# A decoder layer on one core: the first block's gate and up products taken together, the sum of squares later, and fewer steps in the recurrence

## The chip, the core and the metric

The kernel runs on one core of a Trainium2 chip. The metric is the time of one execution on the device in microseconds (us). Six parts of the core matter here. TensorE (PE) multiplies matrices, and its weight loads (PEld) overlap the products. VectorE (DVE) and ScalarE (ACT) work element by element. GpSimd (POOL) does small things and issues some transfers. SyncE (SP) issues most of the DMA transfers, in order. A transfer's landing is told to the engines by a semaphore.

## The reference, cut to what matters

A layer of 256 tokens and 2048 features in float32: a feed-forward part, a mixer that runs attention over a sliding window beside a recurrence (RWKV-7), an attention over a memory, a second feed-forward part, and a last norm. What the change touches:

```python
def rms_norm(x, g):
    return x * rsqrt(mean(x * x) + 1e-6) * g

def swiglu(h, w_gate, w_up, w_down):          # 2048 -> 5632 -> 2048
    return (silu(h @ w_gate) * (h @ w_up)) @ w_down

x = x + 0.5 * swiglu(rms_norm(x, ffn1_norm), ffn1_w_gate, ffn1_w_up, ffn1_w_down)
...
w_log = -softplus(-(w0 + tanh(xw) @ w2)) - 0.5      # decay of the recurrence
a = sigmoid(a0 + xa @ a2)
S = S * w_t + (S @ a_t) * b_t + v_t * k_t           # for each of 256 tokens, 16 heads of 64
y_t = S @ r_t
```

## The kernel before

**Products in three passes.** A float32 product is made of three TensorE products of split operands: each operand is a high part (rounded to TensorE's format, float32r) and a low part (the rest), and `times` (L428) multiplies weight high by feature high (L431), weight low by feature high (L432) and weight high by feature low (L433). Features are the operand that is loaded into TensorE (128 features by 128 tokens), weights stream by 512 columns. Tokens come in two halves, `t` 0 and 1.

**Weights.** `weight_plan` (L106) lists every product in order with its columns. A product is cut into items of two chunks (`KU`) of 128 rows. `load` (L294) issues an item's transfers on SP, `divide` (L362) splits it: ACT casts the high part (L333), DVE subtracts for the low part (L334). `next_item` (L381) issues loads some items ahead and splits up to two single items, or one paired item, ahead of use. A single item has one weight. A paired item has two weights in a tile `raw2` of four chunks, of which there are three buffers; outside the feed-forward's pairs, one such tile holds two single items.

**Two kinds of product.** `product` (L399) multiplies one weight into two banks, one for each half of the tokens. `product_pair` (L489) multiplies gate and up together into several banks; for the items in `SEVEN` it uses seven products in place of eight, of sums of the operands (`sums` L346, `combinations` L443), and for the others the plain eight. In before, the first block of 512 columns of each feed-forward part is two calls of `product` (L760 and L765: gate, then silu, then up, then the product of both), and all later blocks are `gate_up` (L560) by `product_pair`.

**The start.** PE multiplies ones eleven times (L201) until the first data are there. x comes transposed as `xT`, sixteen chunks of features in four tiles; `features` (L682) scales a chunk by the norm's gain and splits it on ACT (L688) and DVE (L689). When all are done, `squares` (L699) squares the four tiles on ACT (L703), adds them up on DVE (L706, L710), and multiplies by a column of ones on PE (L715) for the sum over features; `rstd` (L721) turns it into the scale that the silu and the gate need at the block's end.

**The order of the work.** The stream of weight products is written out in order. All else is in generators, which `Interleave` (L61) moves on by a step whenever the stream calls `tick`, every six products; a `yield` ends a step, `idle(n)` lets n ticks pass. The groups are stepped in a fixed order. The order in which the program states its operations is their rank. The compiler then puts each engine's instructions in order by that rank among those it thinks ready, and each engine works its own list in order. `by_turns` (L170) keeps a list of small products in order, and with `late` it ties them behind the newest product of the stream.

**The recurrence.** It is done in blocks of 128 tokens, `c` 0 and 1, and in two halves of the heads, `h`. `decay_and_rate` (L1054) makes decay and rate in four bursts of products (L1068), each with four sigmoids on ACT (L1079), with two idle ticks between bursts. `values` (L1240) multiplies the values (L1247) and, a step later, the bonus (L1255). `chain` (L1354) makes three masked products for each block (`masked`, L1379: products on PE at L177, then a mask on DVE at L1387), and between them `known`, `solved`, `turned`, `results`, the state of the second block (L1462, L1467), each a step on PE that needs the last one's result. `invert` (L1271) makes the inverse that `solved` needs, with many products of 32x32 and 64x64 (L1295). PSUM has four single banks (`acc`) and two double ones (`two`); masked products, transposes (L185) and the paired products p3, p5, p6 and p7 take double ones.

## Time and profile before

| what | value |
|---|---|
| time, median of 3 runs | 2233.66 us (2233.21 to 2236.87) |
| time of the profiled execution | 2233.47 us |
| its span, first to last instruction | 2231.7 us |
| mean granted clock of TensorE | 0.998 |
| weights' casts on ACT, L333 | 769, 763.4 us |
| weights' low parts on DVE, L334 | 770, 883.2 us |
| moved by DMA | 433.31 MB, mean 194 GB/s |

The span is what the profile's times count from. A row of the timeline gives start, duration, engine, line, operation, tiles (out<-in), shape and count, and in brackets the idle time before it and what ended it. A row of the waits gives who waited for whom, the total in us, the number of times, and the longest. Line numbers are those of the kernel before.

### The profile page before, as it was taken

Reading aid. Unit: us, or ns where it says so; the run is one execution under the profiler, and the core shown is the slowest. Engines: PE = TensorE matmul, PEld = TensorE weight load, DVE = VectorE, ACT = ScalarE, POOL = GpSimd, SP = SyncE. Lnnn points to the kernel's source line nnn. Section 1 sums busy time; section 2 is a strip of 40 time slices with the busy share of each in tenths; the row PEclk is TensorE's granted clock in tenths of the full one; section 3 lists DMA queues with packets and bytes.
Section 4 is the critical chain, followed back from the end, with each engine's and each line's share of the span. In section 5 each row is a group of like instructions: output and inputs, shape, how many; then the busy total and the mean of one; then the engine's idle time right before and its main releaser. Section 6 shows DMA issues by size and latency. Waiting matters only on the chain.

```text
span 2231.7 us, 28333 instructions
## 1 busy us (share of the span) xinstructions
PE 2216.3 (99%) x10792; PEld 1821.0 (82%) x10792; DVE 1747.3 (78%) x2038; ACT 1193.5 (53%) x1436; POOL 71.9 (3%) x139
## 2 busy tenths in 40 slices
PE   9999999999999999999999999999999999999998
PEld 7788888888888877888888888888888888888886
DVE  7988988898987567977545576558888988898987
ACT  6555555555555557544443445556555555555554
POOL 1000000000000000010400000001000000000000
PEclk9999999999999999999999999999999999999999
DMA  7666666565656545677624766657665665565664
GB/s 246 200 226 189 216 195 199 191 207 189 207 184 216 166 137 149 211 230 224 178 63 136 230 223 201 188 162 263 198 203 184 207 202 194 189 203 194 207 205 153
DMA packets 220424, 433.31 MB, mean 194 GB/s; under 512 B 13840, under 2 KB 16224, under 8 KB 220288
## 3 DMA queue, kind: packets, MB, share of 16 engines
q1 hardware_dynamic: 213088, 410.70, 57.9%
q0 software_dynamic: 6624, 20.14, 3.0%
q8 instruction: 84, 1.38, 0.3%
q10 hardware_dynamic: 576, 0.66, 0.1%
q14 instruction: 52, 0.43, 0.1%
HBM read 419.00 MB, written 12.45 MB: 193 GB/s over the span
## 4 chain that ended last, share of the span: by engine, by line
PE 93%; DVE 3%; DMA 1%; issue 1%; ACT 1%; SPq 0%; POOLq 0%; POOL 0%; DVEq 0%; ACTq 0%
PE acc L431 20%; PE acc L432 20%; PE acc L433 20%; PE two L431 8%; PE two L432 8%; PE two L433 8%; PE two L185 2%; DVE lo L334 1%; PE two L177 1%; DMA raw<-in_ffn_w_up_dram 1%; DMA raw<-in_ffn_w_gate_dram 1%; PE two L1295 0%; DVE tlo L359 0%; PE acc L1432 0%; PE acc L1397 0%
## 5 line engine op out<-in xcount | busy, mean ns | idle before, releaser
L333 ACT CAST hi<-raw 128x1024 fp32r<-128x1024 f32 (+1 forms) x769 | 763.4, 1002 | 792.0 <-PE acc L433 372.1
L334 DVE TENSOR_TENSOR lo<-raw,hi 128x1024 fp32r<-128x1024 f32 (+1 forms) x770 | 883.2, 1156 | 338.4 <-ACT hi L333 337.5
L431 PE MATMUL acc<-hi,xhi 128*128 128x512 f32 (+1 forms) x1256 | 493.4, 394 | 0.8 <-ACT xhi L688 0.7
L432 PE MATMUL acc<-lo,xhi 128*128 128x512 f32 (+1 forms) x1256 | 488.1, 389 | 1.2 <-DVE lo L334 1.1
L433 PE MATMUL acc<-hi,xlo 128*128 128x512 f32 (+1 forms) x1256 | 486.8, 388 | 0.0
L431 PEld LDWEIGHTS acc<-hi,xhi 128*128 128x128 f32 x1256 | 236.0, 188 | 56.1 <-issue 6.3
L432 PEld LDWEIGHTS acc<-lo,xhi 128*128 128x128 f32 x1256 | 236.1, 188 | 52.1 <-DVE lo L334 4.0
L433 PEld LDWEIGHTS acc<-hi,xlo 128*128 128x128 f32 x1256 | 236.1, 188 | 47.4
L359 DVE TENSOR_TENSOR tlo<-raw,thi 128x1024 fp32r<-128x1024 f32 x160 | 192.9, 1218 | 0.5 <-ACT thi L358 0.5
L358 ACT CAST thi<-raw 128x1024 fp32r<-128x1024 f32 x160 | 165.9, 1051 | 39.5 <-DVE raw L353 20.9
L432 PE MATMUL acc<-lo,hhi 128*128 128x512 f32 x424 | 166.4, 392 | 0.0
L433 PE MATMUL acc<-hi,hlo 128*128 128x512 f32 x424 | 165.2, 390 | 0.0
L431 PE MATMUL acc<-hi,hhi 128*128 128x512 f32 x424 | 159.9, 391 | 0.0
L431 PE MATMUL two<-hi,xhi 128*128 128x512 f32 x320 | 126.0, 394 | 0.0
L432 PE MATMUL two<-lo,xhi 128*128 128x512 f32 x320 | 124.7, 390 | 0.0
L433 PE MATMUL two<-hi,xlo 128*128 128x512 f32 x320 | 124.6, 389 | 0.0
L353 DVE TENSOR_TENSOR raw<-raw 128x1024 f32<-128x1024 f32 x80 | 97.5, 1219 | 18.5 <-DMA raw<-in_ffn_w_up_dram 16.2
L432 PEld LDWEIGHTS acc<-lo,hhi 128*128 128x128 f32 x424 | 79.6, 188 | 19.2 <-DVE lo L334 3.0
L431 PEld LDWEIGHTS acc<-hi,hhi 128*128 128x128 f32 x424 | 79.1, 188 | 18.7 <-ACT hi L333 2.6
L433 PEld LDWEIGHTS acc<-hi,hlo 128*128 128x128 f32 x424 | 79.6, 188 | 16.3
L431 PEld LDWEIGHTS two<-hi,xhi 128*128 128x128 f32 x320 | 60.1, 188 | 13.8 <-DVE u L583 0.4
L433 PEld LDWEIGHTS two<-hi,xlo 128*128 128x128 f32 x320 | 60.1, 188 | 12.6
(380 smaller groups left out, 3178.8 us busy)
## 6 DMA issues: line engine op xcount, KB each, us to landing
raw<-in_ffn_w_gate_dram SPq DMA_DIRECT2D x167, 512.0 KB, 3.9
raw<-in_ffn_w_up_dram SPq DMA_DIRECT2D x160, 512.0 KB, 4.8
raw<-in_ffn_w_down_dram SPq DMA_DIRECT2D x152, 512.0 KB, 4.8
raw<-in_w_in_dram SPq DMA_DIRECT2D x136, 512.0 KB, 4.0
raw<-in_w_out_dram SPq DMA_DIRECT2D x32, 512.0 KB, 4.2
raw<-in_ffn_w_down_dram SPq DMA_DIRECT2D x12, 1024.0 KB, 5.2
raw<-in_ffn_w_up_dram SPq DMA_DIRECT2D x8, 1024.0 KB, 7.2
raw<-in_w_proj_attn_dram SPq DMA_DIRECT2D x16, 512.0 KB, 4.1
```

What stands on the lines that cost most here:

```text
L177: prev = pe.matmul(to, lhs, rhs, **how)
L185: prev = pe.transpose(to, src, ident[:])
L333: newest["act"] = act.copy(hi[:, s], raw[:, s])
L334: newest["dve"] = dve.tensor_tensor(lo[:, s], raw[:, s], f32(hi[:, s]), ALU.subtract)
L353: dve.tensor_tensor(ta[:], raw[:, 1:3], raw[:, 0:2], ALU.subtract)
L358: act.copy(hi[:, s], t[:])
L359: dve.tensor_tensor(lo[:, s], t[:], f32(hi[:, s]), ALU.subtract)
L431: pe.matmul(o, xh, hi, start=first, stop=False, **how)
L432: pe.matmul(o, xh, lo, start=False, stop=False, **how)
L433: newest["pe"] = pe.matmul(o, xl, hi, start=False, stop=last, **how)
```

## The change

Four things change. The first feed-forward part's first block becomes one `product_pair` of gate and up, without the sevens (`first_block`); the second feed-forward part keeps its two products. Its first item is loaded in four pieces, in the order gate, up, gate, up; the other three loads of the start are whole paired items; the item-by-chunk order of the first single item goes. The multiplications by ones before the start are ten instead of eleven. In `squares` the last products come four steps after the fold instead of one, tied behind the newest product, for x in a double bank. In the recurrence, the idle ticks between the two bursts of a half's decay go (four follow them), the step between the two products of `values` goes, that between the first two masked products goes, and the second block's first masked product moves ahead of `results(0)`, beside `turned`, so that a step less follows it.

```diff
--- before.py
+++ after.py
@@ -87,12 +87,14 @@
         self.until(lambda: not any(q for _, q in self.groups.values()))
 
 
-def feed_forward_plan(wg, wu, wd):
+def feed_forward_plan(wg, wu, wd, together):
     for gi, (j0, nj) in enumerate(GROUPS):
         for j in range(j0, j0 + nj):
-            if j == 0:
+            if j == 0 and together:
+                yield (wg, wu), 0, KD, (0, 0), ()
+            elif j == 0:
                 for w in (wg, wu):
-                    yield w, 0, KD, j * 512, 512
+                    yield w, 0, KD, 0, 512
             else:
                 yield (wg, wu), 0, KD, (j * 512, j * 512), SEVEN
         for n in (0, 2):
@@ -107,7 +109,7 @@
 
 
     w = {n: v[0] for n, v in a.items() if "_w_" in n or n.startswith("w_")}
-    yield from feed_forward_plan(w["ffn1_w_gate"], w["ffn1_w_up"], w["ffn1_w_down"])
+    yield from feed_forward_plan(w["ffn1_w_gate"], w["ffn1_w_up"], w["ffn1_w_down"], True)
     yield None
     w_in = w["w_in"]
     cols = [ATTN_W, 0, 512]
@@ -134,7 +136,7 @@
     for n in range(4):
         yield w["w_cross_o"], 0, 4, n * 512, 512
     yield None
-    yield from feed_forward_plan(w["ffn2_w_gate"], w["ffn2_w_up"], w["ffn2_w_down"])
+    yield from feed_forward_plan(w["ffn2_w_gate"], w["ffn2_w_up"], w["ffn2_w_down"], False)
 
 
 @with_exitstack
@@ -198,7 +200,7 @@
 
     newest = {}
     idle_bank = acc()
-    for _ in range(11):
+    for _ in range(10):
         pe.matmul(idle_bank[:, :P], ones[:], ones[:], start=True, stop=True)
 
     def select(out, in_, pattern, op, fill, base, mult):
@@ -300,6 +302,14 @@
             raw = raws[i] = at["pool"].tile(
                 [P, 2 * KU, 512], F32, tag="raw2", name="raw2", bufs=RAW
             )
+            for j, queue in pieces or ():
+                if j is None:
+                    queue()
+                    continue
+                v, c, r = (w[j in (1, 2)], c0[j in (1, 2)], (k + j // 2) * P)
+                queue.dma_start(raw[:, j], v[r : r + P, c : c + 512])
+            if pieces:
+                return
             rows = slice(k * P, (k + KU) * P)
             for v, c, to in zip(w, c0, (raw[:, 0:4:3], raw[:, 1:3])):
                 newest["load"] = nc.sync.dma_start(
@@ -364,15 +374,16 @@
             return
         raw = raws[i]
         if not paired(i):
-            parts[i] = split_raw(raw, EACH if i < AHEAD else WHOLE, i == 0)
+            parts[i] = split_raw(raw, WHOLE)
         elif items[i][4]:
             t = sums(raw)
             u1, g1 = split_raw(raw[:, 2:4], WHOLE)
             g0, _ = split_raw(raw[:, 0:2], ONE)
             parts[i] = (g0, g1, u1), t
         else:
-            g0, u0 = split_raw(raw[:, 0:2], WHOLE)
-            u1, g1 = split_raw(raw[:, 2:4], WHOLE)
+            how = WHOLE if i else EACH
+            g0, u0 = split_raw(raw[:, 0:2], how, i == 0)
+            u1, g1 = split_raw(raw[:, 2:4], how)
             parts[i] = (g0, u0), (g1, u1)
 
     def cost(i):
@@ -410,12 +421,6 @@
         for k in range(0, nk - KU * len(skewed), KU):
             bg.until(lambda: all(k + i in x.done for i in range(KU)))
             u = next_item()
-            if at["item"] == 1:
-                for i in range(KU):
-                    for t in range(2):
-                        multiply(o[t][:, :n], x, u, k, t, nk, (i,))
-                    bg.tick()
-                continue
             for t in range(2):
                 multiply(o[t][:, :n], x, u, k, t, nk)
                 bg.tick()
@@ -432,9 +437,9 @@
         pe.matmul(o, xh, lo, start=False, stop=False, **how)
         newest["pe"] = pe.matmul(o, xl, hi, start=False, stop=last, **how)
 
-    def multiply(o, x, u, k, t, nk, chunks=range(KU)):
+    def multiply(o, x, u, k, t, nk):
         s = slice(t * P, (t + 1) * P)
-        for i in chunks:
+        for i in range(KU):
             times(
                 o, [x.at(p, k + i)[:, s] for p in range(2)], u[i],
                 k + i == 0, k + i == nk - 1,
@@ -588,6 +593,22 @@
         product_pair(x, c, w, False, SEVEN, EARLY, after, end, finish)
         return hb
 
+    def first_block(sp, x, norm, w):
+        hb = sp.tile([P, 2, 512], F32, tag="hb", name="hb", bufs=2)
+
+        def finish(to, b):
+            bg.until(lambda: norm.r is not None)
+            t = to in ("p4", "p5")
+            if to in ("p2", "p4"):
+                act.activation(hb[:, t], b[to], AF.Silu, scale=norm.r[t])
+            else:
+                dve.scalar_tensor_tensor(
+                    hb[:, t], b[to], norm.r[t], hb[:, t], ALU.mult, ALU.mult
+                )
+
+        product_pair(x, None, w, False, (), (), None, None, finish)
+        return hb
+
     def down(sp, h, c, w, xs, then):
 
 
@@ -708,14 +729,18 @@
                 return
             yield
             dve.tensor_tensor(total[:, :2], total[:, :2], total[:, 2:], ALU.add)
-            yield
-            b = acc()
-            for t in range(2):
-                for k in range(2):
-                    pe.matmul(
+            yield from idle(4)
+            b = two()[:, 0] if whole else acc()
+            by_turns(
+                [
+                    (
                         b[:, t : t + 1], total[:, k, t * P : (t + 1) * P], ones[:, :1],
-                        start=t + k == 0, stop=t + k == 2, skip_group_check=True,
+                        dict(start=t + k == 0, stop=t + k == 2, skip_group_check=True),
                     )
+                    for t in range(2) for k in range(2)
+                ],
+                late=True,
+            )
             self.r = rstd(b[:, :2].unsqueeze(2))
 
     def rstd(ss):
@@ -757,9 +782,14 @@
                     if j == j0 + nj - 1:
                         bg.spawn("feat", c["next"].pop())
                     continue
+                if not last:
+                    hb = first_block(sp, norm.x, norm, wg)
+                    bg.spawn("feat", transposed(hb, 0))
+                    continue
                 pg = product(norm.x, wg)
+                hb = sp.tile([P, 2, 512], F32, tag="hb", name="hb", bufs=2)
+
                 bg.until(lambda: norm.r is not None)
-                hb = sp.tile([P, 2, 512], F32, tag="hb", name="hb", bufs=2)
                 for t in range(2):
                     act.activation(hb[:, t, :], pg[t], AF.Silu, scale=norm.r[t])
                 pu = product(norm.x, wu)
@@ -820,22 +850,17 @@
         pair = sp.tile([P, 8, T], F32, tag="thi", name="xt")
         turned = [v[:] for v in turned] + [pair[:, :4], pair[:, 4:]]
         load(0, (
-            (slice(0, 1), nc.sync),
+            (0, nc.sync),
             (None, lambda: act.dma_start(turned[0][:, :1], a["xT"][:, :1])),
+            (1, nc.sync), (3, nc.sync),
             (None, lambda: nc.sync.dma_start(turned[0][:, 1:2], a["xT"][:, 1:2])),
-            (slice(1, 2), nc.sync), (slice(2, 4), nc.sync),
+            (2, nc.sync),
         ))
         act.copy(junk_t[:, :1], ones[:, :1])
         nc.sync.dma_start(turned[0][:, 2:], a["xT"][:, 2:4])
-        load(2, (
-            (slice(0, 2), nc.sync),
-            (None, lambda: nc.sync.dma_start(turned[1], a["xT"][:, 4:8])),
-            (slice(2, 4), nc.sync),
-        ))
-        for n in range(2, 4):
+        for n in range(1, 4):
+            load(n)
             nc.sync.dma_start(turned[n], a["xT"][:, 4 * n : 4 * n + 4])
-            if n < 3:
-                load(2 * n)
         for n in range(4):
             bg.spawn("feat", n1.features(n, turned[n], turned[0], True))
         bg.spawn("const", late_vectors())
@@ -1080,7 +1105,7 @@
                                 dst[:, q + i, :], b[:, e, i * T : (i + 1) * T], AF.Sigmoid,
                                 bias=bias[:, c : c + 1],
                             )
-                    yield from idle(2)
+                yield from idle(4)
             for h in range(2):
                 for c in range(4):
                     dve.tensor_tensor_scan(
@@ -1249,7 +1274,6 @@
                         start=True, stop=True,
                     )
             act.copy(vtok[h][:], b[:])
-            yield
             b = two()
             for i in range(2):
                 pe.matmul(
@@ -1445,7 +1469,6 @@
                 return t
 
             masked(0, 0)
-            yield
             masked(0, 1)
             yield from wait_for(f"inverse{h}")
             yield
@@ -1454,6 +1477,7 @@
             yield
             solved(0)
             bk = turned()
+            masked(1, 0)
             yield
             results(0)
             b = acc()
@@ -1465,8 +1489,6 @@
                     )
             s0 = wide("s0")
             dve.tensor_tensor(s0[:], b, decays[:], ALU.mult)
-            masked(1, 0)
-            yield
             masked(1, 1)
             yield
             known(1)
```

## The prediction

> **What bounds the kernel.** I read the page first: the busy shares, then the chain that ended last.
>
> ```profile
> span 2231.7 us, 28333 instructions
> PE 2216.3 (99%) x10792; PEld 1821.0 (82%) x10792; DVE 1747.3 (78%) x2038; ACT 1193.5 (53%) x1436; POOL 71.9 (3%) x139
> ...
> PE 93%; DVE 3%; DMA 1%; issue 1%; ACT 1%; SPq 0%; POOLq 0%; POOL 0%; DVEq 0%; ACTq 0%
> ```
>
> TensorE (PE) is busy for 99% of the span and is 93% of the chain. The change removes no product of the layer, so it can gain only where PE waits or loses its pace. Such places are short. Next I therefore read what PE waited for, in the first 62 us, where the first block lies.
>
> ```profile
> PE acc L715 <- DVE xt L710: 1.6, 1, 1.6
> PE acc L202 <- POOL ones L197: 1.1, 1, 1.1
> PE acc L432 <- DVE lo L334: 0.8, 2, 0.5
> PE acc L431 <- ACT xhi L688: 0.7, 1, 0.7
> ```
>
> The longest wait is the sum of squares (L715), then the weights' and features' parts. The last view is the order of time. The profiled run took 2233.47 us for its span of 2231.7, so 1.8 us lie around it; its time is 0.19 below the median of 2233.66. All sums below start from 2233.47.
>
> **The first block, start.** From the timeline of the first 30 us, all engines, then of PE alone:
>
> ```profile
> 1.06 4.99 PE L202 MATMUL acc<-ones 128*128 128x128 f32 x22 [1.06 <-POOL ones L197]
> ...
> 5.77 0.51 PE L431 MATMUL acc<-hi,xhi 128*128 128x512 f32 x1
> ...
> 11.13 1.05 ACT L333 CAST hi<-raw 128x1024 fp32r<-128x1024 f32 x1 [0.42 <-DMA raw<-in_ffn_w_gate_dram]
> ...
> 12.21 1.23 DVE L334 TENSOR_TENSOR lo<-raw,hi 128x1024 fp32r<-128x1024 f32 x1 [0.71 <-ACT hi L333]
> ...
> 12.69 1.71 ACT L688 ACTIVATE xhi<-xt,g_first 128x256 fp32r<-128x256 f32 x4 [0.51 <-DMA xt<-in_xT_dram]
> ...
> 13.26 0.50 PE L431 MATMUL acc<-hi,xhi 128*128 128x512 f32 x1
> ...
> 18.09 2.00 ACT L333 CAST hi<-raw 128x1024 fp32r<-128x1024 f32 x2 [1.08 <-DMA raw<-in_ffn_w_gate_dram]
> ```
>
> ```profile
> 28.45 0.39 PE L431 MATMUL acc<-hi,xhi 128*128 128x512 f32 x1
> 28.67 0.39 PE L432 MATMUL acc<-lo,xhi 128*128 128x512 f32 x1
> ```
>
> Between two products in full flow lie 28.67 - 28.45 = 0.22 us, over longer stretches 0.2275 (0.39 is a duration that overlaps the next). The block has 8 x 2 x 12 = 192 products in both versions. In before, an item (two chunks of one weight, 0.52 MB) feeds 12 products; afterwards an item is two chunks of both weights (1.05 MB) and feeds 24. The 25th product starts at 13.26 in before, the 85th at 28.45: 15.2 us for 60 products that take 13.65, so 1.5 us of waits lie between them, while loads and features arrive just in time.
>
> After the change the second item's first half is cast whole, from a gate chunk and an up chunk, so both of its transfers must have landed. Up to there 1.05 MB of the first item, 0.52 of features and 1.05 of the second item have to come, 2.62 MB. The rows show when before had as much: at 11.13 the wait for six gate chunks ends (with four of features 2.10 MB), at 12.69 that for four feature chunks more (2.62 MB). So: landed 12.7, cast 1.05, PE goes on at about 13.85. The low part (1.23) is ready at 15.1; eight of the half's twelve products use the high part alone, 1.8 us, so it comes in time. Then each item lasts 24 x 0.2275 = 5.46 us. The third item needs 4.19 MB; before had 4.72 at 18.09, which by the slope from 12.69 puts it at 16.8, ready at 17.9, wanted at 19.3. No wait from there on. The 85th product then starts at 13.85 + 60 x 0.2275 = 27.5, **0.95 us earlier** than in before. Neighbouring landings are 1.5 us apart, which I take as the error of 12.7: from 2.45 earlier to 0.55 later.
>
> The idle matmul less is 4.99/22 x 2 = 0.45 us by its two records. I cost it at nothing: PE starts earlier, and then waits for the second item all the same. If item two came early enough, its 0.45 would show; that is inside the bounds above. The item order on the loads' queue (SP) changes too: load four now waits there for the first item's buffer, ahead of the last features, but these are wanted by the seventh item, about 41 us.
>
> **The sum of squares.** From the timelines of PE and of DVE:
>
> ```profile
> 30.94 0.39 PE L433 MATMUL acc<-hi,xlo 128*128 128x512 f32 x1
> 32.92 1.05 PE L715 MATMUL acc<-ones,xt 128*128 128x1 f32 x8 [1.60 <-DVE xt L710]
> ```
>
> ```profile
> 32.19 0.68 DVE L710 TENSOR_TENSOR xt<-xt 128x512 f32<-128x512 f32 x1
> ```
>
> PE stands from 30.94 + 0.23 = 31.17 to 32.92, **1.75 us**. Everything behind L715 on PE, the whole weight stream, stood with it. Afterwards the eight matmuls come three steps of the background work later. A step is issued every six products, so 18 x 0.2275 = 4.1 us, and they are tied behind the newest product. In items they fall in the sixth, near 38 us, 5 us after the fold at L710 is done. The scale that follows is wanted only at the block's end, near 50 us. I take the whole 1.75; bounds 0 (DVE 5 us later) and 1.9. The same edit for the memory's norm meets no wait in before and is worth nothing.
>
> **The block's end.** PE, then windows (length, then busy us and records of PE, PEld, DVE, ACT, POOL, then granted clock, DMA share, GB/s), then DVE and SP:
>
> ```profile
> 55.73 0.61 PE L431 MATMUL acc<-hi,xhi 128*128 128x512 f32 x2
> 56.48 0.50 PE L432 MATMUL acc<-lo,xhi 128*128 128x512 f32 x1
> ```
>
> ```profile
> 35.00:40.00 5.00, 5.00 (x24) 4.12 (x23) 3.33 (x5) 3.38 (x6) 1.10 (x1) 1.00 0.27 104
> 40.00:45.00 5.00, 5.00 (x24) 4.14 (x23) 3.22 (x5) 1.75 (x2) 0.00 (x0) 1.00 0.66 210
> ...
> 44.00:62.00 18.00, 17.86 (x83) 14.42 (x82) 17.92 (x25) 9.73 (x11) 0.00 (x0) 1.00 0.60 190
> ```
>
> ```profile
> 45.37 1.23 DVE L353 TENSOR_TENSOR raw<-raw 128x1024 f32<-128x1024 f32 x1
> ```
>
> ```profile
> 40.56 0.46 SPq L305 DMA_DIRECT2D raw<-in_ffn_w_up_dram  x1
> ```
>
> At 55.73 two products take 0.75 instead of 0.455, and 0.1 more is lost behind them: 0.4 us, for DVE's low part. DVE is full from 44 to 62 (17.92 of 18) but idle for 3.4 us between 35 and 45: the first paired item with sums was issued only at 40.56, and its first DVE step ran at 45.37. With pairs from the start the buffer cycle is that of the later blocks, the load goes out when item six is split (about 35), and DVE can use that idle time. I take **0.4 gained**. The other bound is 1 us lost, since PE now arrives 3 us earlier at a stretch where DVE has no spare time, and the last up bank must be read before the next block gets it.
>
> **The joined steps.** PE's timeline, at the decay, then at the second half's masked products, then at the first half's:
>
> ```profile
> 840.80 0.39 PE L433 MATMUL acc<-hi,xlo 128*128 128x512 f32 x1
> 841.12 1.13 PE L177 MATMUL two<-xs,wa 64*128 64x256 f32 x8
> 842.19 0.50 PE L431 MATMUL acc<-hi,xhi 128*128 128x512 f32 x1
> 842.52 0.40 PE L432 MATMUL acc<-lo,xhi 128*128 128x512 f32 x1
> ```
>
> ```profile
> 1168.56 1.16 PE L177 MATMUL two<-at,aa 64*128 64x128 f32 x16
> 1171.23 1.16 PE L177 MATMUL two<-rt,aa 64*128 64x128 f32 x16
> ```
>
> ```profile
> 1112.39 1.16 PE L177 MATMUL two<-at,aa 64*128 64x128 f32 x16
> 1113.62 1.16 PE L177 MATMUL two<-rt,aa 64*128 64x128 f32 x16
> ```
>
> PE does not wait at these steps; it loses at each crossing between small products and the stream. A decay burst takes 842.52 - 840.80 - 2 x 0.2275 = 1.27 us, of which 842.19 - 841.12 = 1.07 is the burst: 0.20 is lost outside it. A masked product alone costs 1171.23 - 1168.56 - 6 x 0.2275 = 1.30; next to another 1.23. So a join saves 0.07 to some 0.35 (the outside loss and the inner entry). I take 0.25 for each of the two joins of the decay, 0.2 for each of three masked ones (the first half's first pair already stands side by side), 0.1 for each of two at the values: 0.5 + 0.6 + 0.2 = **1.3 us**, bounds 0.4 and 2.5. The eight sigmoids that now follow at once hold ACT, but weights are split two items, 5.5 us, ahead.
>
> **The sum.** 0.95 + 1.75 + 0.4 + 1.3 = 4.4 us. 2233.47 - 4.4 = 2229.1 us. What a measurement here can tell from no change is 0.2%, 4.5 us: faster means below 2229.2, slower above 2238.1. The forecast is a gain that lies on that line.
>
> **The rivals.** First, the start gives nothing: DVE, full from 44 us, holds PE where it stood, and the 3.1 us of the first three terms are waited out there. Then only the joins remain: 2233.47 - 1.3 = 2232.2. For it speaks 17.92 of 18, against it the 3.4 idle us before. Second, the joins save nothing, since PE's order follows readiness and not the steps: 2233.47 - 3.1 = 2230.4. The pair at 1112.39 shows steps that joined unasked. The others lie on the slow side or the fast side by the clock:
>
> ```profile
> 1135.66:1139.07 3.41, 3.41 (x60) 2.63 (x61) 1.23 (x1) 1.07 (x2) 0.89 (x2) 1.00 0.71 235
> 1139.07:1142.49 3.42, 3.42 (x89) 3.38 (x82) 0.99 (x2) 0.93 (x3) 0.00 (x0) 1.00 0.02 5
> 1142.49:1145.90 3.41, 3.41 (x15) 2.38 (x15) 0.53 (x2) 2.06 (x5) 0.00 (x0) 0.50 0.00 0
> 1145.90:1149.31 3.41, 3.41 (x49) 3.22 (x49) 1.23 (x1) 1.88 (x2) 0.00 (x0) 1.00 0.09 11
> ```
>
> In the recurrence the granted clock is 0.50 for one stretch of 3.41 us, just after one filled with small products. At half pace it costs up to 1.7 us. Third, the changed order avoids it, or item two lands early: 2229.1 - 1.7 = 2227.4. Fourth, **slower**: denser bursts, with fewer full products between them, lower the clock in more stretches. Before has one among the 35 stretches from 1092 to 1212; three more give 2234.2, slower than before, and six more 2239.3, slower by over 0.2%. [...]
>
> [...]
>
> **Chances.** The forecast 0.42, split evenly by the line; the third rival 0.24, faster; the first 0.16 and the second 0.11, within; the fourth 0.07, of which 0.05 is over the bound. With a little of the second below the line, faster is 0.48, the same 0.47, slower 0.05. The range goes from 2226.0 (the third with joins at their upper bound, 2227.4 - 1.2, rounded down) to 2233.5 (start and joins at nothing); the fourth and half of the tail below are left out.
>
> **What would show it.** The start: the second item's first product near 13.85, waiting for ACT's cast, and none after. The squares: L715 near 38 us, with no wait. The end: no product near 53 us waiting for L334. The joins: four decay bursts become two, and masked products stand beside transposes and each other. The clock: the count of stretches at 0.50. The prediction is wrong if item two lands after 14.5, if DVE's idle time between 35 and 45 stays, or if more clock stretches fall.

## The result, and the profile after

| what | before | after |
|---|---|---|
| time, median (lowest to highest) of 17 executions each | 2234.28 us (2231.03 to 2237.1) | 2229.66 us (2228.26 to 2231.34) |
| ratio, 95% interval | | 0.998, 0.9973 to 0.9988 |
| time and span of the profiled execution | 2233.47, 2231.7 us | 2228.26, 2226.5 us |

The changed kernel is 4.6 us faster; 2229.1 had been forecast. The total hides errors of both signs, so I read the profile of after in the same order. This profile is of the fastest of its 17 executions, so differences between the two profiles come out somewhat larger than those between the medians. In the changed kernel L343 is the cast of weights on ACT (L333 in before), L344 the low part on DVE (L334), and L436 to L438 are the three products (L431 to L433). Its page, busy time and chain first:

```profile
span 2226.5 us, 28338 instructions
...
PE 2212.4 (99%) x10790; PEld 1820.2 (82%) x10790; DVE 1746.7 (78%) x2038; ACT 1193.4 (54%) x1436; POOL 70.9 (3%) x139
...
PE 97%; DVE 1%; ACT 1%; DMA 0%; issue 0%; POOLq 0%; POOL 0%; SPq 0%; ACTq 0%; DVEq 0%
```

PE is still busy for 99% and is now 97% of the chain, so what changed is again to be found in short places. What PE waited for in the first 64 us (waiter, who was waited for, total, times, longest):

```profile
PE acc L436 <- ACT hi L343: 2.0, 2, 1.3
PE acc L204 <- POOL ones L199: 1.1, 1, 1.1
PE acc L437 <- DVE lo L344: 0.8, 2, 0.5
PE acc L436 <- ACT xhi L709: 0.3, 1, 0.3
```

The wait for the sum of squares is gone. The longest is now for ACT's cast of weights, twice. The timeline of PE says where:

```profile
5.72 0.50 PE L436 MATMUL acc<-hi,xhi 128*128 128x512 f32 x1 [0.33 <-ACT xhi L709]
...
12.80 0.73 PE L436 MATMUL acc<-hi,xhi 128*128 128x512 f32 x2 [1.27 <-ACT hi L343]
...
14.06 0.50 PE L437 MATMUL acc<-lo,xhi 128*128 128x512 f32 x1 [0.29 <-DVE lo L344]
...
27.11 0.39 PE L436 MATMUL acc<-hi,xhi 128*128 128x512 f32 x1
...
37.99 0.95 PE L179 MATMUL two<-ones,xt 128*128 128x1 f32 x8
...
54.82 0.74 PE L436 MATMUL acc<-hi,xhi 128*128 128x512 f32 x2 [0.70 <-ACT hi L343]
...
56.75 0.50 PE L437 MATMUL acc<-lo,xhi 128*128 128x512 f32 x1 [0.49 <-DVE lo L344]
...
839.13 2.00 PE L179 MATMUL two<-xs,wa 64*128 64x256 f32 x16
...
853.51 1.09 PE L187 MATMUL two<-ident,tok 128*128 128x128 f32 x8 [0.41 <-ACT tok L905]
...
1163.31 1.16 PE L179 MATMUL two<-at,aa 64*128 64x128 f32 x16
1164.31 1.06 PE L179 MATMUL two<-rt,aa 64*128 64x128 f32 x16
```

The second item's first product comes at 12.80, the 85th product at 27.11, the squares (now L179) at 37.99 without a wait, and the masked products stand side by side. New are two waits at the block's end (54.82 and 56.75), and one behind the joined decay (853.51).

The cleanest ledger is the start of one and the same instruction in two timelines. The table gives how much earlier (negative) it is than in before's profile, for after and for five experiments of the next section. "Product" counts the stream's 512-column products; the others are transposes on PE. An asterisk marks the interval in which a profile had a stretch of 3.41 us at half clock; before's own lies between 1086 and 1296.

| instruction, us in before | after | block only | joins only | no joins | no block | not late |
|---|---|---|---|---|---|---|
| 85th product, 28.45 | -1.34 | -1.31 | -0.27 | -1.02 | -0.36 | -0.93 |
| 145th product, 44.84 | -3.17 | -3.15 | +1.35* | -2.86 | -2.17 | -2.77 |
| transpose, 168.69 | -1.91 | -2.06 | +1.30 | -2.06 | +1.85* | -1.24 |
| transpose, 827.40 | -1.99 | -1.88 | +1.26 | -2.16 | +1.65 | -1.26 |
| transpose, 1085.80 | -2.13 | -1.88 | +1.12 | -2.16 | +1.50 | -1.41 |
| transpose, 1296.02 | -4.15 | -1.80* | -0.88 | -3.58 | -0.46 | -3.42 |
| last product, 2222.71 | -4.91 | -1.93 | -1.05 | -3.20 | 0.01 | -3.44 |

Down the column of after: 3.17 us are gained by the 145th product, 1.26 are lost at the block's end, 0.14 are gained over the decay, and 2.02 in the recurrence, where before has its half-clock stretch and after none. Behind 1296 only the sum of squares for the memory was changed, and by 1500 the columns still stand where they stood at 1296, to within 0.1. What moves behind that (-0.76 here, +0.38 without the joins) is scatter of single executions: the starts part near 1835 and 1918 us, where PE waits for DVE's low part in some profiles (0.3 us in before, 0.6 in no joins) and not at all in after. So tenths below that have to be settled by where they fall in a timeline, not by the sum.

### The profile page after: what moved, and what is told of

Read it like the earlier page. It is cut to its first block, busy times and chain, and to the rows that moved or that the text cites. A ratio compares the mean times of both kernels' runs of the same rounds, so it can differ in the third digit from the quotient of the medians.

```text
span 2226.5 us, 28338 instructions
## 1 busy us (share of the span) xinstructions
PE 2212.4 (99%) x10790; PEld 1820.2 (82%) x10790; DVE 1746.7 (78%) x2038; ACT 1193.4 (54%) x1436; POOL 70.9 (3%) x139
## 4 chain that ended last, share of the span: by engine, by line
PE 97%; DVE 1%; ACT 1%; DMA 0%; issue 0%; POOLq 0%; POOL 0%; SPq 0%; ACTq 0%; DVEq 0%
PE acc L436 21%; PE acc L437 21%; PE acc L438 21%; PE two L437 9%; PE two L436 9%; PE two L438 9%; PE two L187 2%; PE two L179 1%; PE two L1319 0%; DVE lo L344 0%; PE acc L1456 0%; DMA raw<-in_ffn_w_up_dram 0%; PE acc L1438 0%; PE acc L1421 0%; PE two L1533 0%
## 5 line engine op out<-in xcount | busy, mean ns | idle before, releaser
L343 ACT CAST hi<-raw 128x1024 fp32r<-128x1024 f32 (+1 forms) x769 | 763.3, 1002 | 788.5 <-PE two L438 369.8
L344 DVE TENSOR_TENSOR lo<-raw,hi 128x1024 fp32r<-128x1024 f32 (+1 forms) x770 | 882.9, 1156 | 331.3 <-ACT hi L343 330.1
L436 PE MATMUL acc<-hi,xhi 128*128 128x512 f32 (+1 forms) x1224 | 479.4, 393 | 2.3 <-ACT hi L343 2.0
L437 PE MATMUL acc<-lo,xhi 128*128 128x512 f32 (+1 forms) x1224 | 474.8, 388 | 0.8 <-DVE lo L344 0.8
L438 PE MATMUL acc<-hi,xlo 128*128 128x512 f32 (+1 forms) x1224 | 474.0, 387 | 0.0
L436 PEld LDWEIGHTS acc<-hi,xhi 128*128 128x128 f32 x1224 | 229.7, 188 | 55.6 <-issue 5.1
L437 PEld LDWEIGHTS acc<-lo,xhi 128*128 128x128 f32 x1224 | 229.9, 188 | 49.8 <-DVE lo L344 2.8
L438 PEld LDWEIGHTS acc<-hi,xlo 128*128 128x128 f32 x1224 | 229.8, 188 | 46.3 <-DVE xlo L710 0.2
L438 PE MATMUL acc<-hi,hlo 128*128 128x512 f32 x424 | 165.2, 390 | 0.0
L436 PE MATMUL acc<-hi,hhi 128*128 128x512 f32 x424 | 159.9, 391 | 0.0
L436 PE MATMUL two<-hi,xhi 128*128 128x512 f32 x352 | 138.4, 393 | 0.0
L438 PE MATMUL two<-hi,xlo 128*128 128x512 f32 x352 | 137.1, 390 | 0.0
L437 PE MATMUL two<-lo,xhi 128*128 128x512 f32 x352 | 137.1, 389 | 0.0
L436 PEld LDWEIGHTS acc<-hi,hhi 128*128 128x128 f32 x424 | 79.1, 188 | 18.9 <-ACT hi L343 2.6
L438 PEld LDWEIGHTS acc<-hi,hlo 128*128 128x128 f32 x424 | 79.6, 188 | 16.2
L436 PEld LDWEIGHTS two<-hi,xhi 128*128 128x128 f32 x352 | 66.1, 188 | 15.0 <-DVE u L588 0.5
L438 PEld LDWEIGHTS two<-hi,xlo 128*128 128x128 f32 x352 | 66.0, 188 | 13.8
```

The source lines that it names most:

```text
L343: newest["act"] = act.copy(hi[:, s], raw[:, s])
L344: newest["dve"] = dve.tensor_tensor(lo[:, s], raw[:, s], f32(hi[:, s]), ALU.subtract)
L436: pe.matmul(o, xh, hi, start=first, stop=False, **how)
L437: pe.matmul(o, xh, lo, start=False, stop=False, **how)
L438: newest["pe"] = pe.matmul(o, xl, hi, start=False, stop=last, **how)
```

## The experiments

Line numbers are each kernel's own, and edits are shown shortened. "At 0.999" counts the executions whose mean granted clock was 0.999; the others had less. A half-clock stretch takes 0.5 x 3.41 / 2230 = 0.0008 from that mean, and the drop behind the last product (0.50 from 2227.9 us on in before, whose last product starts at 2222.71) counts in it too, so it sorts executions roughly.

| run | median us | before beside it | ratio, interval | at 0.999 |
|---|---|---|---|---|
| no block | 2232.05 | 2233.48 | 0.9991, 0.9983 to 1.0 | 6 of 11 |
| not late | 2229.72 | 2233.48 | 0.9985, 0.9976 to 0.9993 | 9 of 11 |
| no joins | 2230.25 | 2233.48 | 0.9988, 0.9979 to 0.9997 | 8 of 11 |
| joins only | 2233.06 | 2233.48 | 0.9997, 0.9988 to 1.0006 | 3 of 11 |
| silu early | 2228.88 | 2233.72 | 0.998, 0.997 to 0.999 | 7 of 8 |
| block only | 2230.74 | 2233.72 | 0.9985, 0.9976 to 0.9994 | 7 of 11 |
| dense | 2229.87 | 2233.72 | 0.9981, 0.9972 to 0.999 | 8 of 11 |
| warm | 2231.2 | 2233.72 | 0.9989, 0.998 to 0.9997 | 9 of 11 |
| eleven | 2228.82 | 2234.12 | 0.9973, 0.9962 to 0.9983 | 6 of 8 |
| each | 2227.82 | 2234.12 | 0.9966, 0.9954 to 0.9979 | 5 of 5 |
| changed again | 2229.41 | 2234.12 | 0.9976, 0.9967 to 0.9986 | 9 of 9 |
| item two late | 2231.63 | 2233.67 | 0.9991, 0.9982 to 1.0 | 5 of 11 |

The theory behind the first runs was that of the prediction: the first block gives some 3 us and the joins about one. The rivals were that the clock gives it, and that DVE or ACT takes it back.

### Undo or do one part

No block: after with the first block as two products again.

```diff
-                    hb = first_block(sp, norm.x, norm, wg)
+                pg = product(norm.x, wg)      # and the plan, loads, splits of before
```

> The changed kernel with the first block as two single products again (late squares, joins and ten ones stay). First theory, from the two traces: the block's pairing gains 1.3 us by its 85th product and gives back about 1.2 us at the block's end, so undoing it alone costs 0 to 1 us: 2229.7 to 2230.7 where the changed kernel has 2229.7. Rival, the step as predicted (0.95 + 0.4 gained for good): 2231.0 or more. In the trace, the waits behind the block's last product (before: 0.4 us) should be small again by both.

The median rises to 2232.05, out of the first theory's range and in the rival's, and the waits at the block's end are not small, though both had them so. The squares come late here too, at 32.86 without a wait, and yet nothing is left of that at the block's end, where PE now stands for DVE's low part:

```profile
32.86 0.95 PE L177 MATMUL two<-ones,xt 128*128 128x1 f32 x8
...
55.91 0.50 PE L432 MATMUL acc<-lo,xhi 128*128 128x512 f32 x1 [1.75 <-DVE lo L334]
```

So with the two products in place, removing the squares' wait only moves it 23 us on. That is what the prediction's first rival said of DVE; it holds for this kernel, not for the paired one.

Not late: after with the last products of the squares one step behind the fold and not tied to the stream.

```diff
-            yield from idle(4)
-            b = two()[:, 0] if whole else acc()
-            by_turns([...], late=True)
+            yield
+            b = acc()
+            for t in range(2): for k in range(2): pe.matmul(...)
```

> The changed kernel with the sum of squares' products one step after the fold again, untied. First theory: PE waits for DVE's fold as before, 1 to 1.8 us, and nothing gives it back: 2230.7 to 2231.5. Rival: DVE holds PE at the block's end, so that the wait returns but the wait at the end shrinks by as much: 2229.7, with less waiting near 54 us.

2229.72, the same as after. The rival had this time, but neither theory had the reason. The wait stays away without the edit that was to remove it:

```profile
38.17 0.95 PE L736 MATMUL acc<-ones,xt 128*128 128x1 f32 x8
```

What took the wait away is the pairing; block only, below, has it without the late edit and without this wait too. The reason is read from the program and was not run by itself: in before, the program had to have `norm.r` at the end of gate's product (L760 to L765), which gives the squares their early rank. `first_block` asks for it only when a bank is finished, at the block's end, so the squares come with the ordinary steps.

No joins, and joins only: after without the edits to decay, values and masked products, and before with only those.

```diff
-                yield from idle(4)
+                    yield from idle(2)        # per burst of the decay
+            yield                             # in values, and between masked(0, 0) and (0, 1)
-            masked(1, 0)                      # back behind results(0)
```

> The changed kernel with the recurrence's steps apart as before. First theory: the crossings cost 0.5 to 0.8 us, and the stretch at half clock in the recurrence (1.5 us in the profiled run of before) comes back in some of the executions: 2230.2 to 2232.0, and the times spread wider than the changed kernel's. Rival, the joins save crossings alone and the clock's fall is chance: 2230.2 to 2230.5, spread unchanged. Rival, nothing: 2229.7.

> The kernel before with the recurrence's steps joined and nothing else. First theory: 0.5 to 2 us faster than before (2234.3): 2232.3 to 2233.8, with a narrower spread than before's. Rival, crossings alone: 2233.5 to 2233.8, spread as before's. Rival, nothing: 2234.3.

Joins only moves the median by 0.4 us, inside its interval, so it cannot tell crossings alone from nothing. No joins is 0.6 above after and fits both of its theories; its profile has no half-clock stretch in the recurrence, so it does not show that the joins keep the clock up. In the ledger the decay gives 0.14 to 0.15 in the profiles with joins (after, joins only, no block, not late) and 0 in no joins and block only. For values and masked products, no joins shows what the missing half-clock stretch alone is worth between 1086 and 1296, 3.58 - 2.16 = 1.42; after has 2.02, so 0.6 is theirs. Together 0.74.

Block only: before with the paired first block alone.

> The kernel before with the first block's pairing alone (early untied squares, eleven ones, the recurrence apart). Theory, from the run with the late squares undone: the wait for the squares goes by the pairing itself, since the scale is then asked for at the block's end and no longer after gate; so the pairing alone brings 1.2 to 1.9 us of work by 170 us and most of the steadier clock: 2230.0 to 2231.0 where before has 2233.5 to 2234.3. Rival: the late squares are needed for it: a wait of over 1 us for the fold shows near 33 to 38 us, and the time is 2232 or more.

2230.74, within its theory. Its ledger is that of after up to 1086 to within 0.25 us, and then stays at -1.9: the block carries nearly all of what the work itself gained.

### The block's end

Behind the wait at 54.82 stands ACT. Its timeline in after, and where before did the same work:

```profile
50.75 1.28 ACT L603 ACT_TABLE_LOAD   x1
52.05 0.69 ACT L603 ACTIVATE hb<-acc,rs 128x512 f32<-128x512 f32 x1
52.63 0.61 ACT L481 CAST chi<-u 128x512 fp32r<-128x512 f32 x1
53.14 0.69 ACT L603 ACTIVATE hb<-acc,rs 128x512 f32<-128x512 f32 x1
53.72 1.04 ACT L343 CAST hi<-raw 128x1024 fp32r<-128x1024 f32 x1
```

```profile
32.43 1.28 ACT L764 ACT_TABLE_LOAD   x1
36.13 0.69 ACT L764 ACTIVATE hb<-acc,rs 128x512 f32<-128x512 f32 x1 [2.42 <-POOL rs L729]
```

In before the load of the silu's table fell into idle time of ACT, in the middle of the block. After the pairing, table, both silus and a cast of features (chi) stand in one row ahead of the cast that the next block wants. Silu early loads the table at the start, where ACT did a copy anyway:

```diff
-        act.copy(junk_t[:, :1], ones[:, :1])
+        act.activation(junk_t[:, :1], ones[:, :1], AF.Silu)
```

> The changed kernel, but the one-element copy with which ACT begins is a silu, so that the silu's table is loaded in ACT's idle time at the start and not at the block's end. Theory: in the changed kernel's profile the table load (1.28 us from 50.75) lies ahead of both silus and of the cast that PE waits for at 53.72 (0.87 lost, then 0.66 for the low part that follows the cast). Without it the waits behind the block's last product shrink by 0.9 to 1.5 us, and the time by as much: 2228.2 to 2228.8. Rival: DVE, not ACT, sets that end, so that the cast comes earlier but the low part does not: less than 0.4 us, 2229.3 or more.

2228.88, just above its theory's range. That is 0.8 below after's 2229.66, but against the before beside each the gains are 4.8 and 4.6, so the medians leave open how much of it is the table. The timeline is clearer. The wait for the cast shrinks from 0.70 to 0.22, and that for DVE's low part behind it is no longer listed:

```profile
54.81 0.73 PE L436 MATMUL acc<-hi,xhi 128*128 128x512 f32 x2 [0.22 <-ACT hi L343]
...
56.20 0.50 PE L437 MATMUL acc<-lo,xhi 128*128 128x512 f32 x1
```

By the starts of the products, less the 0.2275 that one takes, PE loses 0.38 + 0.13 at these two in place of 0.87 + 0.66: the table was 1.0 of the loss. (The starts themselves are little earlier, because this execution was 0.5 late before the block's end: its 85th product comes at 27.61, and 27.11 in after.) The rival said that the low part would not come sooner; its product starts at 56.20 in place of 56.75. What is left is not the silus: here ACT itself stood for 0.66 us ahead of that cast, for a buffer that PE still read (PE acc L438).

DVE, which the prediction had as the suspect, did use its idle time. Its windows in after (third busy figure):

```profile
35.00:40.00 5.00, 5.00 (x27) 4.26 (x27) 4.57 (x8) 2.62 (x3) 0.71 (x1) 1.00 0.61 211
40.00:45.00 5.00, 5.00 (x23) 4.12 (x23) 4.64 (x7) 2.66 (x4) 0.02 (x1) 1.00 0.62 211
44.00:62.00 18.00, 16.81 (x77) 13.20 (x76) 16.99 (x26) 10.38 (x13) 0.00 (x0) 1.00 0.52 174
```

4.57 and 4.64 against 3.33 and 3.22, and 16.99 of 18 later against 17.92.

### The start

Eleven: after with eleven idle multiplications. Each: after with the table loaded early, and the second item cast and subtracted by single chunks, as the first one is. Changed again is after itself, beside both.

```diff
-    for _ in range(10):                        # eleven
+    for _ in range(11):
-            how = WHOLE if i else EACH         # each, with the early table
+            how = EACH if i < 2 else WHOLE
```

> The changed kernel with eleven multiplications by ones at the start, as before, in place of ten. Theory: nothing changes at the 85th product (about 27.1 to 27.6 us) nor in the median (within 0.5 us of the changed kernel), since PE waits for the second item's up half all the same; the second item's first product stays near 12.8 to 13.3. Rival: the idle matmul less was part of the start's gain, and putting it back costs 0.2 to 0.45 us at both places and in the median.

> The changed kernel with the silu's table loaded at the start, and the second item cast and subtracted chunk by chunk instead of in halves of two chunks. Theory: PE goes on with the second item's gate chunk before its up half has landed and been cast, so the 25th product comes at 11.5 to 12.0 instead of 12.8 to 13.3, and the 85th 0.6 to 1.0 us earlier (26.3 to 26.9); what is gained there is still there at the 385th product, and the median is 0.3 to 1.0 below that of the changed kernel with the early table alone (2228.9), about 2228.2. Rival: the up chunks hold PE a few products later, or DVE, which then works four short steps more, gives the gain back at the block's end; the 85th product or the 385th stays where it was and the median stays at 2228.9.

> The changed kernel once more, on the same chip and in the same rounds as the two beside it, so that tenths of a us can be compared. Both theories: 2229.2 to 2230.1 in the median; the wait for the cast at the block's end (0.7 to 1.0 us near 54) in the profile again, the second item's first product between 12.6 and 13.3 by the landing of its up half.

Eleven: the second item's first product at 13.02, as in changed again (13.02), and a median of 2228.82 against 2229.41. Putting the idle matmul back costs nothing. The 85th product can't be compared, since a half-clock stretch from 14.87 to 18.28 lies ahead of it in this profile; it starts at 28.94.

Each: the 25th product comes at 11.63, the 85th at 26.30, the 385th at 98.17 (changed again 13.02, 27.34, 99.83). The waits of its first 64 us:

```profile
PE acc L204 <- POOL ones L199: 1.1, 1, 1.1
PE acc L436 <- ACT hi L343: 0.7, 1, 0.7
PE acc L437 <- DVE lo L344: 0.2, 1, 0.2
```

The wait for the second item is gone. Against silu early, which has 99.20 at the 385th product, 1.0 us of that is kept. The median of 2227.82 is 1.6 below changed again, with four of five executions below the latter's fastest (2228.15). It is the fastest kernel of all, 6.3 us below before. How the 1.6 divides between the early table and the chunks rests on the timelines; the chunks were not run without the early table.

### Denser steps, and the clock

Dense: after with five more steps of the recurrence joined, to see whether more joins gain more or cost clock (the prediction's slow rival).

```diff
             masked(0, 2)
-            yield                              # likewise behind (1, 0), (1, 1), (1, 2), solved(1)
```

> The changed kernel with five more steps of each half's recurrence joined (after both remaining masked products of the first block's results, after the second block's, and after solved). Theory: a join is worth some 0.1 us where it saves a crossing, so 10 joins save up to 1 us, less what PE then waits for ACT and DVE: 2228.9 to 2229.7, and the clock as in the changed kernel. Rival, the fourth of the prediction: denser small products let the clock fall in the recurrence: a stretch at half clock between 1090 and 1210 us, 2231 or more, and most executions with the lower mean clock.

2229.87: no gain, 0.2 above its theory's range and well below the rival's. There is no half-clock stretch in its recurrence. But PE now waits for the mask that DVE puts on a masked product, since no other step lies between:

```profile
1168.82 1.35 PE L1528 MATMUL two<-xs,g 128*128 128x256 f32 x5 [1.58 <-DVE mk L1411]
```

Warm: before with PE multiplying eight more times 128 columns (a result that nothing uses) where it stood for the squares.

```diff
+    [(b[:, P : 2 * P], total[:, 2, :P], ones[:])] * 8   # ahead of the four of L715
```

> The kernel before with eight products of 128 columns more, directly ahead of the sum of squares' own, so that PE multiplies where it stood for 1.75 us; their result is not used. Theory: PE's standing in the first block is what makes the clock fall in some executions (at 33.7 us in the profile of the run with joins alone), so the undisturbed time stays, 2232.1, but more executions have the higher mean clock (12 of 33 so far) and the median falls by 0.5 to 1.2 us. Rival: the falls have nothing to do with this wait: the share stays at a third, the median within 0.3 us of before's.

2231.2, 2.5 below before, although the squares are no sooner needed: no half-clock stretch in its profile, and 9 of 11 executions at 0.999, where before has 30 of 94 over the four comparisons of this section. But the expectation that the undisturbed time stays failed: among executions at 0.999 the mean is 2231.25, and 2232.61 in before beside it. So of the 2.5 about 1.4 is not the clock. The profile has a better start (85th product at 27.25 against 28.45), ahead of the place that was edited; why is open.

Where did the clock fall? All seven stretches in the fourteen profiles (behind the first products and ahead of the last) take 3.41 us, at 0.50. Five lie in the first block, and each follows a stretch of the same length in which PE was busy for 1.81 us or less, about half of the time or under. Here are three of the five, no block, joins only and eleven (length, then PE's busy us first, granted clock third from the end):

```profile
54.14:57.56 3.42, 1.67 (x8) 1.13 (x8) 3.42 (x5) 1.32 (x3) 0.00 (x0) 1.00 0.16 53
57.56:60.98 3.42, 3.42 (x14) 2.93 (x13) 3.09 (x4) 1.01 (x2) 0.00 (x0) 0.50 0.93 301
```

```profile
30.25:33.66 3.41, 1.81 (x13) 1.35 (x12) 2.96 (x7) 2.33 (x2) 0.00 (x0) 1.00 0.59 180
33.66:37.08 3.42, 3.42 (x10) 2.65 (x10) 2.10 (x4) 1.21 (x3) 1.77 (x1) 0.50 0.68 261
```

```profile
11.46:14.87 3.41, 1.55 (x6) 0.99 (x7) 1.87 (x2) 2.95 (x5) 0.00 (x0) 1.00 1.04 403
14.87:18.28 3.41, 3.41 (x10) 2.65 (x9) 3.34 (x8) 1.94 (x4) 0.00 (x0) 0.50 1.03 393
```

Dense has 1.56 ahead of its fall at 14.60, item two late (below) 0.36. Of the stretches of 3.41 us in before's first block, counted from the first entry of the clock in its trace, at 5.85 us, the one with the least busy time was not followed by a fall:

```profile
29.74:33.16 3.42, 1.82 (x9) 1.21 (x9) 3.42 (x6) 1.78 (x2) 0.00 (x0) 1.00 0.73 246
```

and in after the least is 2.06, at 11.74, also without a fall behind it. So much the same wait for the second item (first product at 13.02 in both) came with a fall in eleven and without one in changed again, and the 85th product then started at 28.94 and at 27.34, 1.6 us apart. What decides between the two was not shown. The last run makes the wait longer:

```diff
+        nc.sync.dma_start(turned[1], a["xT"][:, 4:8])
         for n in range(1, 4):
             load(n)
-            nc.sync.dma_start(turned[n], a["xT"][:, 4 * n : 4 * n + 4])
+            if n > 1: nc.sync.dma_start(turned[n], a["xT"][:, 4 * n : 4 * n + 4])
```

> The changed kernel with four chunks of features (0.52 MB) sent ahead of the second item, so that this lands about 1.4 us later and TensorE's wait for it grows from 1.4 to 2.8 us. It tests what makes the clock fall in the first block. [...] So the median rises by 1.4 and by about 1.6 for the half clock besides, 3.0 together, to about 2232.5, and most executions have a mean clock of 0.998 where the changed kernel had it in 3 of 26; a profile shows the half-clock stretch within 14 to 19 us, behind a stretch with at most 1.8 of 3.41 busy. Rival: the falls come by chance and not by the wait; then the median rises by the 1.4 alone, to 2230.9, and some nine executions in ten keep 0.999.

The outcome lies between the two. The second item's first product comes at 14.57, 1.55 to 1.77 later than in the two profiles of after, and the profiled execution has the fall:

```profile
11.24:14.65 3.41, 0.36 (x3) 0.08 (x1) 0.53 (x3) 1.17 (x2) 0.00 (x0) 1.00 1.05 402
14.65:18.07 3.42, 3.42 (x8) 2.53 (x9) 3.19 (x5) 1.86 (x2) 0.00 (x0) 0.50 1.04 395
```

But the median rises by 2.0 to 2.2 (from 2229.66 and 2229.41), not by 3.0, and not by the rival's 1.4 either. 6 of 11 executions are below 0.999, where after has 3 of 26. With the longer wait lower mean clocks were thus more frequent, but the 3.0 rested on the author's estimate that nearly every execution would have a fall, and that was not shown.

## Why the prediction was right, and where it was not

**The start**, 0.95 forecast. 1.34 between the two profiles. The mechanism is the one named: PE waits for the second item's cast and for nothing after it. The sizes moved: its first product came at 12.80, not 13.85, as the up half landed at 11.63, not 12.7, within the error of 1.5 that was put on it. Then PE waited 0.46 more for DVE's low part, which had been called in time: of the eight products that the prediction ran ahead of it, only three did (12.80 and 13.38 above). But one pair is not the term: the 85th product starts at 27.25, 28.09, 28.18 and 28.45 in the four profiles with the old block, mean 27.99, and between 27.11 and 27.61, mean 27.36, in the six with the new one, its split as in after and no half-clock stretch ahead. So the term is 0.6 to 1.3. The idle matmul at nothing: eleven agrees.

**The sum of squares**, 1.75 forecast. The place (37.99, "near 38"), the missing wait and the size (3.17 - 1.34 = 1.83) are right, the reason is not. The step that failed is "afterwards the eight matmuls come three steps of the background work later": that edit is worth nothing (not late, 2229.72), and the pairing, by where it asks for `norm.r`, does it. Nor was there a margin of 5 us: the fold itself moved to the time of the products, in not late to 37.32 + 0.68 = 38.00 against the products at 38.17.

**The block's end**, 0.4 gained forecast; 1.26 lost. This is the term with the wrong sign. The step said "DVE can use that idle time", and DVE did. It failed by looking at one engine alone: the silus and their table moved too, from idle time of ACT at 32 to 36 us to a place right ahead of a wanted cast at 51 to 54, and silu early takes 1.0 of the loss away. The bound of 1 us lost named the bank of up, not ACT.

**The joins**, 1.3 forecast, 0.74 measured. Values and masked products: 0.6 of 0.8. Decay: 0.14 of 0.5. A joined burst lasts 2.00 us (839.13 above) against two of 1.13, and crosses to the stream once: from the product at 838.81 to the second one behind it at 841.40, less two products, it costs 2.14 against 2 x 1.27. So the joined bursts did save 0.4 each, and 0.76 is gained when both are done. Of this 0.62 is lost at one transpose (853.51 above): it starts 0.56 us later than the product ahead of it (852.72) allows, of which the view shows 0.41 as idle. What failed is "weights are split two items, 5.5 us, ahead": not weights stood behind the eight sigmoids, but a scaling of tokens (L905), which the transpose needs. ACT's last sigmoid and the scaling in after:

```profile
851.78 0.52 ACT L1104 ACTIVATE aa<-two,v_rwkv 128x256 f32<-128x256 f32 x1
852.14 1.32 ACT L905 ACTIVATE tok<-acc,rs 128x512 f32<-128x512 f32 x2
```

The wait is there in all kernels with the joined decay, 0.40 to 0.41, and in none without it.

**The clock**, which the sum had left out and the third rival had priced at 1.7 us. After's profile has no half-clock stretch before its last product; before's has one. Executions at 0.999 are 23 of 26 for after and 30 of 94 for before. Among these alone the means are 2229.43 and 2232.29, 2.9 us apart; the means of all the 26 and 94 are 2229.56 and 2233.99, 4.4 apart. So about 2.9 us is work and waits, and about 1.6 is a clock that falls in fewer executions. This is a sorting by the mean clock and not an experiment, and it is rough, as said above. By the terms, 0.6 to 1.3, 1.83, -1.26 and 0.74 make 1.9 to 2.6, so 0.3 to 1.0 of the 2.9 is in no term.

That the forecast of 2229.1 came out to 0.6 us is thus in part luck: the clock's gain, seen as a rival, made up for the block's end and half of the joins. Of the three signs of being wrong none came: item two was there by 12.80, DVE's idle time between 35 and 45 shrank from 3.4 to 0.8, and fewer clock stretches fell. But the sign for the block's end, no product that waits for the low part, failed. The first rival was near the truth in what it said of the block's end, 1.3 of the first 3.2 us given back, but not in its cause, DVE. The second was half right. The fourth, slower by clock falls in the recurrence, was not seen: the two falls there (before and block only) belong to kernels without the joins, and dense has none there; nor have no joins and warm, also with the steps apart.

What makes the clock fall stays open. In the first block each of the five falls came behind a stretch in which PE was busy for 1.81 of 3.41 us or less. The two in the recurrence did not: the one in block only comes, as in before (3.42 of 3.42 us busy), behind a stretch full of small products:

```profile
1136.94:1140.35 3.41, 3.41 (x105) 3.37 (x97) 0.69 (x2) 1.22 (x3) 0.00 (x0) 1.00 0.02 7
1140.35:1143.76 3.41, 3.41 (x12) 2.37 (x12) 0.84 (x2) 1.49 (x4) 0.00 (x0) 0.50 0.02 5
```

Why it fell there, and why the same place is passed without a fall in the other profiles, the runs do not show.

## What to carry to other kernels

When a step is moved, follow each engine that it uses to the new place: here a table load and two silus moved from idle time to a place ahead of a cast that PE waited for, the block's end lost 1.3 us, and loading the table at the start gave 1.0 of it back. A wait of TensorE can come with a cost beyond its length: here the five falls of the clock in the first block came behind stretches of 3.41 us in which PE was busy for 1.81 us or less, and a half-clock stretch cost 1.4 to 1.6 us. So remove such waits first, and judge tenths by many executions, since a single profile can hold or lack such a stretch. When an item must land before use, split its first casts as finely as its transfers arrive: on top of the early table that was worth about 1 us here.

## What the runs showed of the hardware that was not expected

- A stretch of 3.41 us with PE busy for about half of it or less came ahead of each of the five falls in the first block: PE was busy there for 1.81 (joins only), 1.67 (no block), 1.56 (dense), 1.55 (eleven) and 0.36 us (item two late). Stretches with 1.82 (before) and 2.06 us (after) were not followed by a fall.
- One stretch at half clock cost less than half of its 3.41 us (1.71): 1.42 in the recurrence of before, by the ledger, and some 1.6 in the first block of eleven.
- ACT's load of a table took 1.28 us and nothing more: the cast ahead of it ended at 50.70, it began at 50.75, and the silu at 52.05.
